# A two-layer trunk on one core: the first layer's MLP in phases, with ten pairs of hidden blocks by seven block products over both token halves

## The chip, the core and the metric

The kernel runs on one core of a Trainium2 chip. Its engines are TensorE (PE, with its weight loads PEld), VectorE (DVE), ScalarE (ACT), GpSimd (POOL) and SyncE (SP, which issues most DMAs). The metric is the device time of one launch in microseconds (us); lower is better.

## The reference

Tokens x (1, 1024, 1024) go through a layer with an mLSTM mixer and an MLP, then through a layer with latent attention and an MLP; a shared K/V is made between. All is float32. Cut to what the change touches:

```python
# layer 0
x = x + gate * rmsnorm(mlstm_mixer(modulate(rmsnorm(x, g), shift, scale), ...), g)
h = modulate(rmsnorm(x, g), shift, scale)
x = x + gate * rmsnorm(jnp.square(jax.nn.relu(h @ mlp_w1[0])) @ mlp_w2[0], g)   # 1024 -> 4096 -> 1024
# shift, scale, gate: columns of silu(c) @ ada_w + ada_b, one row for all tokens
# shared K/V from x, then layer 1: the same frame around causal latent attention, and an MLP
```

## The kernel before, in words

Activations stand transposed, features on 128 partitions and tokens along the row, in two token halves of 512 (`hfs[0]`, `hfs[1]`; H = 512). A float32 product is done as three matmuls (`mm3`, L230): each operand is split into a rounded part `hi` and a rest `lo`, and lo*hi, hi*lo and hi*hi are added in PSUM. A weight block of 128x1024 (512 KB) is loaded into a `raw` buffer (a ring of four that weights, background loads and others share), `wsplit` casts it on ScalarE (L189, `wh`) and subtracts on VectorE (L190, `wl`).

`mlp` (L941) walks a list of steps. A `hidden` step makes one block of 128 hidden features for a half: 8 x 3 matmuls of 128x512 into one PSUM tile `ps`, then ReLU and square on ScalarE and a split. An `up` step multiplies hidden blocks by the second weight and adds into y: 24 matmuls into `pm`, and two additions of 128x1024 (L198). Loads run two steps ahead (AHEAD). The generator yields "within" in the middle of a step and a step's name at its end.

Other work is placed between steps by generators. `go` makes each instruction of TensorE follow the one before it in the program's order, so TensorE's list is fixed. `two_streams(dense, other, fill)` runs `other`; where that yields a number n it lets the dense stream go on for 2n half steps. When the dense stream ends first, the rest of `other` is run with nothing between. `behind(fill, per)` is such an `other`: it takes `per` steps of `fill` and then yields 1.

Background work: the modulation rows (shift, scale, gate) are sums over c times ada_w. `ada_chunk` (L346 on) makes one of 512 columns: four loads of 512 KB, one multiply (L358) and seven dependent multiply-adds (L360) on VectorE into `tma` (one buffer), then four transposes on TensorE (L340) and a reduce (L342). `bg_latent` holds the sums for the shared K/V and `latent_weights` (L1130): six blocks folded with scale and shift, whose shift sums are transposed at L1154 and reduced at L1155. `bg_rest` holds four parts of two sums each for layer 1.

In layer 0, half 0's MLP `mlp(0, hfs[0], z0, [4]*8)` runs first, its first 20 yields beside `post` of half 1 (residual and norm, `p1`), the rest beside `bg_latent`. Half 1's MLP `mlp(0, hfs[1], z1, [2]*14+[4])` is the dense stream beside `mixer1` of half 0, which is half 0's latent attention, with `bg_rest` as fill. There the attention's scores (L1325 to L1331), softmax and the transposes of the probabilities (L1445) have one dense step, 24 matmuls, between scores and transposes.

## Time and profile before

| what | value |
|---|---|
| times of three runs | 2396.41, 2397.75, 2398.75 us |
| median | 2397.75 us |
| span of the profiled execution | 2395.7 us (2.05 us less than the median) |
| granted TensorE clock, mean | 0.997 |
| busy PE, DVE, ACT, POOL | 2364.8, 1550.3, 1054.9, 18.3 us |
| DMA | 374 MB, mean 156 GB/s |

The page gives for each engine its busy time and its share of the span. The page's span starts at the first instruction and ends with the last; the runs' time includes what lies around it. Matmuls overlap in the pipeline, so a group's mean duration is longer than the step from one start to the next. In a row of the groups stand line, engine, operation, names out<-in, shapes, count, then busy us, mean ns, and the idle time before with what ended it.

### The profile page before, as it was taken

How to read it: one execution, taken by the hardware profiler on the slowest of the kernel's cores; microseconds unless marked ns; L12 is line 12 of the kernel's file. 1: busy time of each engine (PE TensorE's matmuls, PEld its weight loads, DVE VectorE, ACT ScalarE, POOL GpSimd, SP SyncE). 2: the span in 40 equal slices, each digit the busy share in tenths (PEclk: the TensorE clock that was granted, in tenths of full speed). 3: DMA queues.
4: the chain of work that ended last, by engine and by line, in shares of the span. 5: the costliest groups of instructions: out<-in, count | busy, mean ns of one | idle time of the engine just before them, and what ended most of it. 6: DMA issues, size and time to landing. Idle time of an engine off the chain costs nothing.

```text
span 2395.7 us, 30518 instructions
## 1 busy us (share of the span) xinstructions
PE 2364.8 (99%) x11621; PEld 1945.5 (81%) x11621; DVE 1550.3 (65%) x2431; ACT 1054.9 (44%) x1712; POOL 18.3 (1%) x91
## 2 busy tenths in 40 slices
PE   7999999999999999999999999999999999999998
PEld 5888888788888887888888877888888888888886
DVE  6667866858656677877764867766566386353345
ACT  4355334655333454444444554344444353443333
POOL 1000000000000000000000000000000000000000
PEclk9999999999999999999999999999999999999999
DMA  8442654544654745545543444864424354354431
GB/s 310 148 143 81 192 178 134 165 132 150 189 171 152 243 138 179 159 160 186 168 137 114 153 162 153 260 240 133 139 97 150 105 167 128 101 189 140 144 99 62
DMA packets 377106, 374.48 MB, mean 156 GB/s; under 512 B 24355, under 2 KB 282464, under 8 KB 376960
## 3 DMA queue, kind: packets, MB, share of 16 engines
q1 hardware_dynamic: 376672, 372.44, 48.9%
q8 instruction: 91, 1.49, 0.3%
q14 instruction: 55, 0.45, 0.1%
q0 software_dynamic: 288, 0.10, 0.0%
HBM read 313.24 MB, written 59.24 MB: 155 GB/s over the span
## 4 chain that ended last, share of the span: by engine, by line
PE 91%; DVE 4%; DMA 3%; ACT 1%; issue 1%; SPq 0%; DVEq 0%; ACTq 0%
PE ps L231 17%; PE ps L232 17%; PE ps L233 17%; PE pm L231 10%; PE pm L232 10%; PE pm L233 10%; PE pc L1445 1%; PE pc L231 1%; PE pc L233 1%; PE pc L232 1%; PE pm L815 1%; PE pm L1331 1%; DMA raw<-in_mlp_w_dram 1%; DVE wl L190 1%; PE pm L1325 1%
## 5 line engine op out<-in xcount | busy, mean ns | idle before, releaser
L190 DVE TENSOR_TENSOR wl<-raw,wh 128x1024 fp32r<-128x1024 f32 (+2 forms) x366 | 438.7, 1202 | 449.5 <-ACT wh L189 442.3
L189 ACT CAST wh<-raw 128x1024 fp32r<-128x1024 f32 (+2 forms) x366 | 376.0, 1032 | 717.0 <-PE ps L231 392.2
L231 PE MATMUL ps<-k,wl 128*128 128x512 f32 x1528 | 611.0, 400 | 2.3 <-ACT k L671 1.4
L233 PE MATMUL ps<-k,wh 128*128 128x512 f32 x1528 | 601.0, 393 | 0.0
L232 PE MATMUL ps<-k,wh 128*128 128x512 f32 x1528 | 600.9, 393 | 0.0
L231 PEld LDWEIGHTS ps<-k,wl 128*128 128x128 f32 x1528 | 287.0, 188 | 69.7 <-issue 2.9
L233 PEld LDWEIGHTS ps<-k,wh 128*128 128x128 f32 x1528 | 287.0, 188 | 67.3 <-issue 0.5
L232 PEld LDWEIGHTS ps<-k,wh 128*128 128x128 f32 x1528 | 287.5, 188 | 63.6 <-issue 1.7
L198 DVE TENSOR_TENSOR k<-k,pm 128x512 f32<-128x512 f32 (+1 forms) x254 | 210.9, 859 | 107.0 <-PE pm L233 106.5
L231 PE MATMUL pm<-hd,wl 128*128 128x512 f32 x512 | 202.0, 394 | 0.4 <-ACT hd L470 0.4
L233 PE MATMUL pm<-hd,wh 128*128 128x512 f32 x512 | 199.8, 391 | 0.0
L232 PE MATMUL pm<-hd,wh 128*128 128x512 f32 x512 | 199.5, 390 | 0.2 <-DVE hd L471 0.2
L231 PE MATMUL pm<-wh,hd 128*128 128x512 f32 x488 | 192.9, 395 | 3.2 <-ACT raw L1337 2.9
L232 PE MATMUL pm<-wl,hd 128*128 128x512 f32 x488 | 191.3, 392 | 0.0
L233 PE MATMUL pm<-wh,hd 128*128 128x512 f32 x488 | 190.3, 390 | 0.0
L360 DVE SCALAR_TENSOR_TENSOR tma<-raw,cond,tma 128x512 f32<-128x512 f32 x168 | 125.6, 747 | 20.6 <-DMA raw<-in_kv_ada_w_dram 14.6
L471 DVE TENSOR_TENSOR hd<-tmp,hd 128x512 fp32r<-128x512 f32 x128 | 88.3, 690 | 56.8 <-ACT hd L470 56.5
L1337 ACT ACTIVATE raw<-pm,sm 128x128 f32<-128x128 f32 (+3 forms) x64 | 47.5, 742 | 151.3 <-DVE sm L1336 122.7
L232 PEld LDWEIGHTS pm<-hd,wh 128*128 128x128 f32 x512 | 96.2, 188 | 21.3 <-DVE hd L471 0.5
L231 PEld LDWEIGHTS pm<-hd,wl 128*128 128x128 f32 x512 | 96.1, 188 | 21.2 <-ACT hd L470 0.8
L233 PEld LDWEIGHTS pm<-hd,wh 128*128 128x128 f32 x512 | 96.1, 188 | 21.1
L231 PEld LDWEIGHTS pm<-wh,hd 128*128 128x128 f32 x488 | 91.6, 188 | 24.9 <-ACT raw L1337 5.5
(347 smaller groups left out, 3414.5 us busy)
## 6 DMA issues: line engine op xcount, KB each, us to landing
raw<-in_mlp_w_dram SPq DMA_DIRECT2D x256, 512.0 KB, 4.1
raw<-in_ada_w_dram SPq DMA_DIRECT2D x80, 512.0 KB, 4.3
raw<-in_a_w_in_dram SPq DMA_DIRECT2D x48, 512.0 KB, 4.1
xs<-k SPq DMA_DIRECT2D x40, 256.0 KB, 4.8
raw<-in_kv_ada_w_dram SPq DMA_DIRECT2D x16, 512.0 KB, 3.8
raw<-in_a_w_out_dram SPq DMA_DIRECT2D x16, 512.0 KB, 4.6
kd<-k SPq DMA_DIRECT2D x32, 256.0 KB, 3.7
vd<-k SPq DMA_DIRECT2D x32, 256.0 KB, 5.0
```

Of the source, the lines that this page charges most:

```text
L189: nc.scalar.copy(hi[:, :n], r[:, :n])
L190: i = nc.vector.tensor_sub(lo[:, :n], r[:, :n], hi[:, :n].bitcast(F32))
L198: return f(*a, **k)
L231: nc.tensor.matmul(o, ll, rh, start=start, stop=False)
L232: nc.tensor.matmul(o, lh, rl, start=False, stop=False)
L233: pe_last[0] = nc.tensor.matmul(o, lh, rh, start=False, stop=stop)
L360: nc.vector.scalar_tensor_tensor(acc, r[:, kk], cond[:, k : k + 1], acc, ALU.mult, ALU.add)
L471: nc.vector.tensor_sub(lo, u, hi.bitcast(F32))
L815: nc.tensor.matmul(nv[:, r, i], hf.PT[p_][:, r, cs], v[:, 2 * p_ + r], start=g == 0, stop=True,)
L1325: nc.tensor.matmul(o[:, :w], ql, kh, start=True, stop=False)
L1331: nc.tensor.matmul(o[:, :w], qh, kh, start=False, stop=True)
L1337: nc.scalar.activation(pr[:, :n], f, AF.Exp, bias=m, scale=SCALE, accum_out=l)
```

## The change

Layer 0's MLP is done in phases.

(A) `up_front` makes the first six pairs of hidden blocks (ALONE = 6, twelve blocks) of half 0 as before and stores each block in DRAM (`hidd`). Beside it runs `post` of half 1, two steps of it for each step, which now also forms sums and differences of the two halves' normed operands (`kept1`) for phase B and stores two tiles in DRAM (`b12`).

(B) `seven` makes the other ten pairs for both halves at once. A pair's product with both halves is seen as 2 x 2 blocks (two hidden blocks, or the two halves of features, by two token halves) and done with seven block products in place of eight, 7 x 12 = 84 matmuls of 128x512 in place of 96. Weight sums (L1009 to L1017 of the new program) and sums of results (L1036, L1044, L1046) are formed on VectorE. After each product one step of the background work `bgl` (`bg_latent`, then `bg_rest`) is taken. Results go to `hidd`.

(C) The down product of half 0 reads the hidden blocks from `hidd` (`mlp(..., stored=True)`, 32 steps of 24 matmuls, `f2`), beside `behind(bgl, 1)`. `with_b12` gets the stored tiles back.

(D) Half 1's MLP, `up_front` of six pairs and then the stored down product, is the dense stream beside `mixer1` of half 0, with `bgl` as fill. The attention yields 0.5 in place of 1: half a dense step, 12 matmuls.

Counted in the two programs: 120 fewer matmuls of 128x512 (11,283 matmuls in all, 11,403 before), 70 more instructions on VectorE, 4 more on ScalarE, and 92 more DMAs issued by SyncE (44 stores to and 64 fetches from `hidd`, 4 for `b12`, 20 fewer weight loads).

What stands in a row, at two places of the program. Names are buffers with numbers; [waits X] names whose semaphores the row waits for.

The first place is the end of half 0's MLP, and the background sums around it. TensorE before: here a sum (tma_1345) of `bg_rest`, beside half 1's MLP.

```order
L232 MATMUL pm_1388_8185<-hd_1290_7648,wh_1357_8027 128x512
L233 MATMUL pm_1388_8185<-hd_1290_7648,wh_1357_8027 128x512
L231 MATMUL pm_1388_8185<-hd_1353_7994,wl_1358_8028 128x512
L232 MATMUL pm_1388_8185<-hd_1353_7994,wh_1357_8027 128x512
L231 MATMUL pc_1376_8125<-k4_1364_8069,wl_1331_7912 128x512 [waits Activation_49]
L233 MATMUL pm_1388_8185<-hd_1353_7994,wh_1357_8027 128x512
L340 MATMUL pc_1389_8199<-ident_64,tma_1345_7971 128x128 [waits DVE_49]
L340 MATMUL pc_1389_8199<-ident_64,tma_1345_7971 128x128 x3
L232 MATMUL pc_1376_8125<-k4_1365_8070,wh_1330_7911 128x512 [waits DVE_49]
L233 MATMUL pc_1376_8125<-k4_1364_8069,wh_1330_7911 128x512
L231 MATMUL pc_1376_8125<-k4_1364_8069,wl_1331_7912 128x512 [waits Activation_49]
```

TensorE after, from the last two matmuls of half 0's down product (pm_1400) to the first two of half 1's hidden blocks (ps_1463):

```order
L233 MATMUL pm_1400_8134<-k4_1386_8002,wh_1395_8074 128x512
L234 MATMUL pm_1400_8134<-k4_1385_8001,wh_1395_8074 128x512
L341 MATMUL pc_1401_8160<-ident_64,tma_1379_7989 128x128 [waits DVE_49]
L341 MATMUL pc_1401_8160<-ident_64,tma_1379_7989 128x128 x3
L341 MATMUL pc_1408_8185<-ident_64,tma_1403_8168 128x128 [waits DVE_49]
L341 MATMUL pc_1408_8185<-ident_64,tma_1403_8168 128x128 x3
L341 MATMUL pc_1415_8210<-ident_64,tma_1410_8193 128x128 [waits DVE_49,PE_49]
L341 MATMUL pc_1415_8210<-ident_64,tma_1410_8193 128x128 x3
L341 MATMUL pc_1422_8235<-ident_64,tma_1417_8218 128x128 [waits DVE_49,PE_49]
L341 MATMUL pc_1422_8235<-ident_64,tma_1417_8218 128x128 x3
L232 MATMUL ps_1463_8320<-k4_1286_7509,wl_1456_8305 128x512 [waits DVE_49]
L233 MATMUL ps_1463_8320<-k4_1287_7510,wh_1455_8304 128x512 [waits Activation_49]
```

Four sums' transposes now stand one after another between the two dense streams, where one stood among matmuls.

VectorE before, part of the sum tma_1345 above, with the MLP's operations (L471, L198, L190) between:

```order
L360 SCALAR_TENSOR_TENSOR tma_1345_7971<-raw_1348_7980,cond_85,tma_1345_7971 128x512 [waits DVE_49]
L360 SCALAR_TENSOR_TENSOR tma_1345_7971<-raw_1349_7984,cond_85,tma_1345_7971 128x512 [waits DMAHW4_49,DVE_49]
L471 TENSOR_TENSOR hd_1353_7994<-tmp_1355_8020,hd_1353_7994 128x512 [waits Activation_49]
L360 SCALAR_TENSOR_TENSOR tma_1345_7971<-raw_1349_7984,cond_85,tma_1345_7971 128x512 [waits DVE_49]
L198 TENSOR_TENSOR k4_1208_7286<-k4_1208_7286,pm_1359_8031 128x1024 [waits PE_49,Pool_49]
L190 TENSOR_TENSOR wl_1352_7991<-raw_1350_7988,wh_1351_7990 128x1024 [waits DMAHW5_49,Activation_49]
L198 TENSOR_TENSOR k4_1209_7287<-k4_1209_7287,pm_1360_8045 128x1024 [waits PE_49,Pool_49]
L190 TENSOR_TENSOR wl_1358_8028<-raw_1356_8025,wh_1357_8027 128x1024 [waits DMAHW6_49,Activation_49]
```

VectorE after, the third of the four sums (tma_1410), from the reduce of the second to its own:

```order
L343 TENSOR_REDUCE sm_1409_8190<-pc_1408_8185 128x4 [waits PE_49]
L359 TENSOR_SCALAR tma_1410_8193<-raw_1411_8194,cond_85 128x512 [waits DMAHW4_49,DVE_49]
L344 TENSOR_TENSOR ada_104<-sm_1409_8190,cols_95 128x4 [waits DVE_49]
L361 SCALAR_TENSOR_TENSOR tma_1410_8193<-raw_1411_8194,cond_85,tma_1410_8193 128x512 [waits DVE_49]
L387 SCALAR_TENSOR_TENSOR mods_106<-ada_104,cols_95 128x8 [waits DVE_49]
L361 SCALAR_TENSOR_TENSOR tma_1410_8193<-raw_1412_8198,cond_85,tma_1410_8193 128x512 [waits DMAHW5_49,DVE_49]
L361 SCALAR_TENSOR_TENSOR tma_1410_8193<-raw_1412_8198,cond_85,tma_1410_8193 128x512 [waits DVE_49]
L361 SCALAR_TENSOR_TENSOR tma_1410_8193<-raw_1413_8202,cond_85,tma_1410_8193 128x512 [waits DMAHW6_49,DVE_49]
L361 SCALAR_TENSOR_TENSOR tma_1410_8193<-raw_1413_8202,cond_85,tma_1410_8193 128x512 [waits DVE_49]
L361 SCALAR_TENSOR_TENSOR tma_1410_8193<-raw_1414_8206,cond_85,tma_1410_8193 128x512 [waits DMAHW7_49,DVE_49]
L361 SCALAR_TENSOR_TENSOR tma_1410_8193<-raw_1414_8206,cond_85,tma_1410_8193 128x512 [waits DVE_49]
L343 TENSOR_REDUCE sm_1416_8215<-pc_1415_8210 128x4 [waits PE_49]
```

The sum's operations stand without dense operations between, and its reduce waits for TensorE.

The second place is the start of half 0's down product, and the folding of the latent weights around it. TensorE before, one transpose of `latent_weights` beside half 0's MLP:

```order
L233 MATMUL pm_1144_6817<-hd_1067_6336,wh_1127_6723 128x512
L231 MATMUL pm_1144_6817<-hd_1077_6409,wl_1128_6724 128x512
L232 MATMUL pm_1144_6817<-hd_1077_6409,wh_1127_6723 128x512
L233 MATMUL pm_1144_6817<-hd_1077_6409,wh_1127_6723 128x512
L1154 MATMUL pc_1145_6843<-ident_64,tma_1132_6758 128x128 [waits DVE_49]
L231 MATMUL ps_1154_6871<-k4_732_4342,wl_1137_6777 128x512 [waits DVE_49]
L232 MATMUL ps_1154_6871<-k4_733_4343,wh_1136_6776 128x512 [waits Activation_49]
```

TensorE after, from the last of the seven-product matmuls (ps_1107) to the first of the down product (pm_1165):

```order
L232 MATMUL ps_1107_6561<-k4_822_4852,wl_1093_6415 128x512
L233 MATMUL ps_1107_6561<-k4_823_4853,wh_1092_6414 128x512
L234 MATMUL ps_1107_6561<-k4_822_4852,wh_1092_6414 128x512
L1327 MATMUL pc_1120_6656<-ident_64,tma_1117_6627 128x128 [waits DVE_49]
L1327 MATMUL pc_1144_6746<-ident_64,tma_1123_6675 128x128 [waits DVE_49]
L232 MATMUL pm_1165_6871<-k4_1136_6710,wl_1134_6706 128x512 [waits DVE_49]
L233 MATMUL pm_1165_6871<-k4_1137_6711,wh_1133_6705 128x512 [waits Activation_49]
L234 MATMUL pm_1165_6871<-k4_1136_6710,wh_1133_6705 128x512
L232 MATMUL pm_1165_6871<-k4_1136_6710,wl_1134_6706 128x512
```

VectorE after, from the first transpose's reduce to the subtraction (wl_1134) that row pm_1165 waits for:

```order
L1328 TENSOR_REDUCE lbias_135<-pc_1120_6656 128x1 [waits PE_49]
L1317 TENSOR_SCALAR tma_1123_6675<-raw_1121_6659,ada_104 128x128 [waits DMAHW7_49]
L490 TENSOR_TENSOR k4_1131_6699<-raw_1129_6697,k4_1130_6698 128x1024 [waits DMAHW6_49,Activation_49]
L1319 SCALAR_TENSOR_TENSOR tma_1123_6675<-raw_1121_6659,ada_104,tma_1123_6675 128x128 [waits DVE_49] x7
L1322 TENSOR_TENSOR raw_1121_6659<-raw_1121_6659,mods_106 128x1024 [waits DVE_49]
L1328 TENSOR_REDUCE lbias_135<-pc_1144_6746 128x1 [waits PE_49]
L490 TENSOR_TENSOR k4_1137_6711<-raw_1135_6709,k4_1136_6710 128x1024 [waits DMAHW4_49,Activation_49]
L190 TENSOR_TENSOR wl_1125_6686<-raw_1121_6659,wh_1124_6685 128x1024 [waits Activation_49]
L190 TENSOR_TENSOR wl_1134_6706<-raw_1132_6703,wh_1133_6705 128x1024 [waits DMAHW2_49,Activation_49]
```

Two transposes stand next to each other where 48 matmuls lay between two, and VectorE has a whole folding (tma_1123), two fetched splits (k4_1131, k4_1137) and the first down weights between them and the down product.

The diff, cut to its core:

```diff
+    def up_front(l, hf, pairs):
...
+        def hidden(f):
+            def hid(w):
...
+                    nc.scalar.activation(s, pt, AF.Relu)
+                    nc.scalar.activation(s, s, AF.Square)
+                    nc.sync.dma_start(hidd[hf.i, f // 2][:, ts(f % 2, 512)], s)
...
+    def seven(l, pairs, B, out):
...
+        def load(p_):
+            with tc.high_priority(PRIO):
+                r1, r2 = raw(), raw()
+                for r, f in ((r1, 2 * p_), (r2, 2 * p_ + 1)):
+                    nc.sync.dma_start(r.rearrange("p (a b) -> p a b", b=P), wcols(w1, f * P))
...
+                A = wsplit(r1, 1024)
+                t1, t2 = raw(), raw()
+                nc.vector.tensor_add(t2[:, lo_], r2[:, lo_], r2[:, hi_])
+                nc.vector.tensor_sub(t1[:, hi_], t2[:, lo_], r1[:, lo_])
...
+        def product(u, i):
...
+            for k in range(4):
+                mm3(o, wh[:, k], wl[:, k], bh[k], bl[k], i in (1, 2, 7) and k == 0, k == 3, more=i not in (1, 2, 7))
...
+            for u, i in ((cur, 1), (prev, 5), (cur, 2), (prev, 4), (cur, 6), (prev, 3), (cur, 7)):
+                if u:
+                    product(u, i)
+                    yield "hid"
+            prev = cur
...
-    def mlp(l, hf, y, sizes, rows=False):
+    def mlp(l, hf, y, sizes, rows=False, stored=False):
...
+        def fetch(f):
+            with tc.high_priority(PRIO):
+                r, hi, lo = raw(), k4v(F32R), k4v(F32R)
+                nc.sync.dma_start(r, hidd[hf.i, f // 2])
+                split_wide(hi, lo, r.rearrange("p (a b) -> p a b", b=512))
...
+        if stored:
+            fetch(0)
+            fetch(2)
+            steps = []
+            for g in range(NF // 4):
+                for i in range(4):
+                    load, run = up(list(range(4 * g, 4 * g + 4)), i, g == NF // 4 - 1)
+
+                    def both(load=load, f=4 * g + 2 * i):
+                        w = load()
+                        if i >= 2 and f < NF:
+                            fetch(f)
+                        return w
+
+                    steps.append((both, run))
...
-        yield 1
+        yield (0.5, 1)[hf.i]
...
-            yield 2
+            yield 1
...
-                hf, groups, cycle((1,)),
+                hf, groups, cycle((0.5,)),
...
-    f0 = mlp(0, hfs[0], z0, [4] * 8)
-    for n in range(20):
-        if next(f0) != "within":
+    for v in up_front(0, hfs[0], range(ALONE)):
+        if v != "within":
+            next(p1, None)
             next(p1, None)
     drain(p1)
-    two_streams(f0, behind(bg_latent(), 4))
+    bgl = chain(bg_latent(), bg_rest())
+    traced = nc.cur_bb.bb.instructions
+    z0 = FH()
+    f2 = mlp(0, hfs[0], z0, [], stored=True)
+    f0, n = seven(0, range(ALONE, NF // 2), blocks, both_halves), 0
+    while go(f0) is not end:
+        pace[0] = next(i for i in reversed(traced) if i.engine == dve)
+        n += 1
+        next(bgl, None)
+        if n == 7 * (NF // 2 - ALONE) - 5:
+            next(f2)
...
+    two_streams(with_b12(f2), behind(bgl, 1))
     rope_perm()
...
-    two_streams(mlp(0, hfs[1], z1, [2] * 14 + [4]), mixer1(hfs[0], z0, attention_first), bg_rest())
+    two_streams(
+        chain(
+            up_front(0, hfs[1], range(ALONE)),
+            (v for v in mlp(0, hfs[1], z1, [], stored=True) if v != "primed"),
+        ),
+        mixer1(hfs[0], z0, attention_first), bgl,
+    )
```

More of the change, by code (lines that the diff above doesn't have):

```diff
@@ L939, with ahead_of @@
     AHEAD = 2
-    def mlp(l, hf, y, sizes, rows=False):
+    hidd = scratch([2, NF // 2, P, 2 * H], "hidd")
+    def ahead_of(steps, primed=False):
+        ready = []
+        for n in range(len(steps) + AHEAD):
+            if primed and n == AHEAD:
+                yield "primed"
+            if n < len(steps):
+                ready.append(steps[n][0]())
+            if n >= AHEAD:
+                yield from steps[n - AHEAD][1](ready.pop(0))
+                yield steps[(n - AHEAD + 1) % len(steps)][1].__name__
@@ new lines, in both_halves, with done @@
+    def both_halves(p_):
+        o, s = Half(), [k4v(), hdv()]
+        o.c = [[s[0][:, 0], s[1][:, 0]], [s[0][:, 1], s[1][:, 1]]]
+        def done():
+            nc.vector.tensor_scalar(s[0], s[0], 0.0, None, ALU.max)
+            nc.vector.tensor_scalar(s[1][:, 1], s[1][:, 1], 0.0, None, ALU.max)
+            for i in range(2):
+                nc.scalar.activation(s[i], s[i], AF.Square)
+                nc.sync.dma_start(hidd[i, p_], s[i].rearrange("p a b -> p (a b)"))
+        o.done = done
+        return o
@@ L1046, in mlp @@
         up = up_rows if rows else up_cols
+        if stored:
[11 more added lines that the diff above has]
+                    steps.append((both, run))
+            n = 0
+            for v in ahead_of(steps, True):
+                if v == "primed":
+                    yield v
+                    continue
+                n += v != "within"
+                yield v if v == "within" else "hid"
+            return
         steps, prev, f0 = [], [], 0
@@ L1757, in post @@
         yield 0
+        if kept:
+            yield from kept(y, rstd)
+            return
         hf.h2 = Split()
@@ L1764, with kept0 @@
     )
-    p0 = post(hfs[0], y0, B0, x_ahead(k4v, True), A1, adac(0, SH2))
+    def kept0(y, rstd):
+        hfs[0].h2 = Split()
+        h = hfs[0].h2
+        yield from normed_kept(y0, rstd, A1, adac(0, SH2), list(zip(h.hi.t, h.lo.t)))
+    p0 = post(hfs[0], y0, B0, x_ahead(k4v, True), A1, adac(0, SH2), kept0)
     so = split_o(hfs[1])
```

159 lines of the change are left out of this document (142 added, 17 removed).

## The prediction

> **What bounds the kernel now.** I read the page's totals and the chain of waits first, then windows of 100 us, then TensorE's waits, and last timelines of the stretches whose pieces the change re-uses. The first fence holds the totals and the chain by engine, the second windows (span, then busy us of PE, PEld, DVE, ACT, POOL with counts; granted clock; DMA share; GB/s), the third TensorE's longest waits (total, times, longest).
>
> ```profile
> PE 2364.8 (99%) x11621; PEld 1945.5 (81%) x11621; DVE 1550.3 (65%) x2431; ACT 1054.9 (44%) x1712; POOL 18.3 (1%) x91
> PE 91%; DVE 4%; DMA 3%; ACT 1%; issue 1%; SPq 0%; DVEq 0%; ACTq 0%
> ```
>
> ```profile
> 0.00:100.00 100.00, 86.87 (x458) 67.14 (x459) 62.33 (x118) 38.09 (x60) 7.31 (x26) 0.97 0.75 254
> 500.00:600.00 100.00, 100.00 (x435) 81.03 (x434) 83.26 (x120) 56.88 (x79) 0.55 (x4) 1.00 0.48 151
> 600.00:700.00 100.00, 100.00 (x448) 81.96 (x447) 64.94 (x85) 36.79 (x48) 0.00 (x0) 1.00 0.63 194
> 1000.00:1100.00 100.00, 99.72 (x522) 83.72 (x521) 75.52 (x129) 46.13 (x84) 0.82 (x4) 1.00 0.58 180
> 1500.00:1600.00 100.00, 99.61 (x477) 82.75 (x476) 65.70 (x101) 40.19 (x63) 0.20 (x1) 1.00 0.79 264
> 2300.00:2396.00 96.00, 87.17 (x382) 71.18 (x380) 46.87 (x78) 30.46 (x55) 0.00 (x0) 0.97 0.23 77
> ```
>
> ```profile
> PE pc L527 <- DMA k<-in_x_dram: 4.4, 4, 1.5
> PE pm L231 <- ACT k L473: 4.4, 1, 4.4
> ```
>
> TensorE is the bound and has no slack to give: of its 30.9 us idle, 13.1 lie in the first 100 us and 8.8 in the last 96, and no wait between is over 4.4 us. So every matmul removed is time gained, and every wait added to TensorE is time lost, one for one.
>
> **What the change removes.** After the change TensorE's list holds 120 fewer matmuls of 128x512 (11,283 for 11,403): ten pairs at 84 for 96. Their price is not the mean duration. The first row below gives that mean (400 ns), the others, TensorE's timeline of 24 such matmuls, give the starts.
>
> ```profile
> L231 PE MATMUL ps<-k,wl 128*128 128x512 f32 x1528 | 611.0, 400 | 2.3 <-ACT k L671 1.4 <-DVE wl L190 0.8
> 1052.79 0.39 PE L231 MATMUL ps<-k,wl 128*128 128x512 f32 x1
> 1053.02 0.39 PE L232 MATMUL ps<-k,wh 128*128 128x512 f32 x1
> ...
> 1058.36 1.04 PE L1445 MATMUL pc<-ident,raw 128*128 128x128 f32 x8
> ```
>
> Twenty-four starts take 1058.36 − 1052.79 = 5.57 us, 0.232 us each: the durations overlap. The gain is 120 × 0.232 = **27.8 us**, not the 48 that 0.400 would give. Also from this: 12 matmuls are 2.78 us, a round of 84 is 19.5 us.
>
> **Prices for what is added.** VectorE's timeline of one background sum, then its groups for operand splits and weight folding, then the loads.
>
> ```profile
> 654.71 0.68 DVE L342 TENSOR_REDUCE sm<-pc 128x4 f32<-128x512 f32 x1
> 655.31 0.48 DVE L358 TENSOR_SCALAR tma<-raw,cond 128x512 f32<-128x512 f32 x1
> 655.70 0.15 DVE L343 TENSOR_TENSOR ada<-sm,cols 128x4 f32<-128x4 f32 x1
> 655.82 0.75 DVE L360 SCALAR_TENSOR_TENSOR tma<-raw,cond,tma 128x512 f32<-128x512 f32 x1
> 658.25 1.23 DVE L190 TENSOR_TENSOR wl<-raw,wh 128x1024 fp32r<-128x1024 f32 x1 [1.68 <-ACT wh L189]
> 659.40 3.11 DVE L360 SCALAR_TENSOR_TENSOR tma<-raw,cond,tma 128x512 f32<-128x512 f32 x4
> 509.72 4.73 DVE L927 SCALAR_TENSOR_TENSOR k<-k,mods,tmc 128x512 f32<-128x512 f32 x7
> 518.57 2.50 DVE L930 TENSOR_TENSOR k<-k,hd 128x512 f32<-128x512 f32 x4
> L1146 DVE SCALAR_TENSOR_TENSOR tma<-raw,ada,tma 128x128 f32<-128x128 f32 x21 | 7.4, 352 | 0.7
> L1149 DVE TENSOR_TENSOR raw<-raw,mods 128x1024 f32<-128x1024 f32 x6 | 7.3, 1225 | 0.2
> L1155 DVE TENSOR_REDUCE lbias<-pc 128x1 f32<-128x128 f32 x6 | 1.7, 283 | 0.0
> raw<-in_mlp_w_dram SPq DMA_DIRECT2D x256, 512.0 KB, 4.1
> raw<-in_ada_w_dram SPq DMA_DIRECT2D x80, 512.0 KB, 4.3
> ```
>
> Start to start that is about 1.15 us for a subtraction of 1024 columns (658.25 to 659.40), 0.77 for a dependent multiply-add of 512 (3.11 / 4), 0.67 for an independent one (4.73 / 7), 0.61 for an add of 512 (2.50 / 4), 0.6 for the reduce, 0.4 for the first multiply.
>
> **1. End of half 0's down product: +26.** The stored `mlp` gives 32 steps, and `behind(bgl, 1)` takes one background step at each: about 4.6 of the eight sums of `bg_rest`. The rest is drained by the same call after the dense work has ended, and the order on record shows it: after the last matmul of pm_1400 TensorE has nothing but four groups of transposes until ps_1463, and each needs a sum that VectorE does after the group before it (tma has one buffer). On VectorE from the last matmul: the addition 1.15, a reduce 0.6, then three sums of 0.4 + 7 × 0.77 = 5.8 each with small operations between (7.1 the first, which has two adds of 512 in it, 6.0 and 5.9 the others), after each about 0.8 for the transposes and the way to TensorE and back and 0.6 for the reduce, and 1.15 for wl_1456 at the end: 1.75 + 19.0 + 3 × 1.4 + 1.15 = 26.1. Before, these sums lay beside half 1's MLP; that cover is gone. Bounds: 22 (no tiny operations between), 31 (12 loads through the four-slot raw ring at 4.3 us, if they don't stay ahead).
>
> **2. From the products to the down product: +8.7.** The first two latent-weight transposes stand behind the last product. Between them and the next matmul VectorE has, in order, a reduce 0.28, a multiply 0.2, a subtraction 1.15, seven multiply-adds of 128x128 at most 0.352 each (0.27 by their pitch), a product of 1.15, a reduce 0.28, and three subtractions of 1.15: 8.4, and 0.3 for the way. Before, 48 matmuls stood between such transposes. Bounds 8 and 9.5.
>
> **3. First steps of the down product: +5.5.** Up to the third step's weights (wl_1161) VectorE has some 14.4 us of folding and splits by the same prices, TensorE 48 matmuls, 11.1 us and two short transposes; then two fetched halves of `hidd` each 1.15 late. 3 to 8.
>
> **4. From plain pairs to products: +4.2.** From post's last column sum to the operand half hd_847 VectorE's list holds 24 operations of 1024, ten adds and ten multiply-adds of 512: 24 × 1.15 + 6.1 + 6.7 + 0.5 = 40.9 us; TensorE has 157 matmuls, 36.4. Bounds 0 (post runs ahead by that much) and 8.
>
> **5. The seven products: +6.** Per pair VectorE has about 16 of TensorE's 20.0 us (19.5 and four background transposes), so it isn't the bound. The ring is: three or four pieces of a round go through one slot after another (a load 4.1, a split 1.15, and again, behind a wait for VectorE's turn), about 21 us against 20. One us lost in each of five rounds with background loads; bounds 0 and 17 (3.4 each, if a load takes 5). The 64 stores and fetches of `hidd` and b12 add DMA work that the window of 600 to 700 at 194 GB/s leaves room for.
>
> **6. Down product, steady: +2.** Per 5.57 us it takes about 2.6 loads of 512 KB: a weight, a background load, and a fetch at nearly every step, since `fetch` in `both` reads `i` when it is called, and that is 3 then: 32 fetches a half where 16 are needed. That is about 245 GB/s; 254 to 264 occurs in the windows above, with TensorE at 99.6 in the later one. Bounds 0 and 10.
>
> **7. Thin filler: +3.** Twelve matmuls (2.78 us) now stand between scores and transposes. In the trace scores end at 1052.79 and VectorE's last probability scaling is the second row here:
>
> ```profile
> 1055.41 0.28 DVE L1339 TENSOR_SCALAR raw<-raw,sm 128x128 f32<-128x128 f32 x1
> 1056.58 0.35 DVE L1339 TENSOR_SCALAR raw<-raw,sm 128x256 f32<-128x256 f32 x1
> ```
>
> It ends at 1056.93, 4.1 us after the scores: 24 matmuls cover that, 12 leave 1.4. There are four such places, four more with heavier scores; without background multiply-adds between, VectorE comes about 1.5 us sooner. Bounds 0 and 10.
>
> **8. Clock: +3.** The windows with 13.1 and 8.8 us idle show 0.97, so about 3 us of full-speed work lost in each; all others show 1.00. The gap of step 1 is longer than either, though broken by transposes. Bounds 0 and 6. [...]
>
> **The sum.** −27.8 + 26.0 + 8.7 + 5.5 + 4.2 + 6 + 2 + 3 + 3 = +30.6. The profiled span is 2395.7, the median of the runs 2397.75, so 2.05 lie around the span, taken as unchanged. 2397.75 + 30.6 gives **2428 us**, 1.3% slower.
>
> **Rivals.**
> - *Faster: the leftover sums stay hidden.* It turns on one place: if the three sums ran beside the last steps of the down product, step 1 falls from 26 to 2, and with the small terms at their low ends (8 + 3) the time is 2397.75 − 27.8 + 13 = 2383. It takes a step-1 gap under about 14 us to end faster. For it: VectorE is only 65% busy. Against: the order puts every one of those sums behind the addition of pm_1400. 0.06.
> - *No change:* steps 1 and 2 near their bounds (22 + 8) and all else hidden: 2397.75 − 27.8 + 30 = 2400. For it: 35% of VectorE is free, and TensorE lost under 0.5 us in each of the four windows above that lie between the ends. 0.10.
> - *Loads bind:* steps 5 and 6 at their upper ends, 27 instead of 8, and 5 us more in step 1: 2452. For it: the ring has four slots and the loads of a round are serial; against: TensorE stayed at 99.6 while 264 GB/s moved. 0.18.
> - The forecast itself, 2405 to 2442: 0.66.
>
> A measurement of this kernel can tell about 0.2%, 4.8 us, from no change. The no-change case reaches 2393 to 2402.5. Below that lies 0.06, above it 0.84. The range of 8 in 10 is 2402 to 2453: from the no-change case's edge to the case of binding loads.
>
> **What would show it.** After: TensorE with 120 fewer matmuls; a hole of 22 to 31 us with four small groups of transposes right after the first half's down product, VectorE on line 361 throughout; before the down product a hole of 8 to 10 with line 1327's transposes; rounds of 20 to 21 us in the products; waits at line 1618 of 0.5 to 1.5. I would be wrong if the line 361 sums run beside matmuls at that place, or if products take over 23 us a round.

## The result, and the profile after

The changed kernel takes 2509.2 us (median of four runs, 2507.1 to 2515.4), the kernel before 2397.4 on the same chip: 1.046 times as long, 95% interval 1.045 to 1.048, or 112 us more. The forecast was 2428, and its range ended at 2453.

The totals of the profile after, in the same form as before:

```profile
span 2505.0 us, 30646 instructions
PE 2374.4 (95%) x11501; PEld 1938.9 (77%) x11501; DVE 1623.3 (65%) x2501; ACT 1086.4 (43%) x1708; POOL 17.3 (1%) x83
```

(ScalarE ran 1708 instructions, four fewer than before and not four more as counted ahead.) The span grew by 109.3 us. TensorE's idle time, span less busy time, grew from 30.9 to 130.6: 99.7. Its busy time grew too, by 9.6, though it has 120 matmuls fewer, worth 27.8 at 0.232: the remaining ones took 37.4 us longer. These two numbers, 99.7 of waits and 37.4 of slower matmuls, are what has to be explained.

Five of the windows of 100 us show where (span, busy us and counts of PE, PEld, DVE, ACT, POOL, granted clock, DMA share, GB/s):

```profile
500.00:600.00 100.00, 93.63 (x397) 75.14 (x395) 76.84 (x95) 54.36 (x77) 0.00 (x0) 0.97 0.44 140
700.00:800.00 100.00, 83.49 (x345) 65.84 (x344) 81.20 (x137) 47.58 (x56) 0.00 (x0) 0.91 0.64 211
800.00:900.00 100.00, 88.86 (x371) 70.19 (x369) 72.87 (x87) 37.50 (x37) 0.00 (x0) 0.93 0.77 251
1000.00:1100.00 100.00, 73.58 (x307) 58.16 (x306) 64.56 (x95) 33.45 (x52) 0.00 (x0) 0.85 0.60 191
1400.00:1500.00 100.00, 88.63 (x358) 70.00 (x357) 74.59 (x87) 40.75 (x51) 0.39 (x4) 0.91 0.62 200
```

TensorE is idle for 100.9 us between 500 and 1500 us, in the phases of the new program, so all of the growth lies there. The granted clock, which was 1.00 everywhere between the ends, is now under 1.00 in each of these five windows.

TensorE's longest waits (engine, line, what it waited for: total, times, longest):

```profile
PE pc L341 <- DVE tma L361: 22.0, 3, 8.4
PE pm L232 <- ACT k L489: 10.6, 3, 5.4
PE pm L232 <- ACT raw L1510: 10.2, 12, 1.3
PE ps L232 <- DVE wl L190: 9.7, 4, 4.5
PE pm L232 <- ACT k L202: 9.1, 1, 9.1
PE pm L232 <- DVE k L198: 8.7, 7, 2.7
PE ps L233 <- DVE hd L490: 6.3, 1, 6.3
PE ps L232 <- ACT hd L1048: 6.1, 3, 2.9
PE pm L232 <- DVE wl L190: 5.9, 1, 5.9
PE pm L233 <- DVE k L490: 5.9, 4, 4.0
PE pc L1327 <- DVE tma L1319: 5.5, 1, 5.5
```

Before, the longest was 4.4 us. Line 341 is the hole that the prediction put at the end of the first half's down product. TensorE's timeline there (start, duration, engine, line, operation, idle time before and what ended it), with the next hidden block's matmuls behind it:

```profile
1010.51 1.12 PE L341 MATMUL pc<-ident,tma 128*128 128x128 f32 x4 [8.41 <-DVE tma L361]
1018.41 1.09 PE L341 MATMUL pc<-ident,tma 128*128 128x128 f32 x4 [6.78 <-DVE tma L361]
1026.27 1.09 PE L341 MATMUL pc<-ident,tma 128*128 128x128 f32 x4 [6.78 <-DVE tma L361]
1031.82 0.80 PE L232 MATMUL ps<-k,wl 128*128 128x512 f32 x1 [4.46 <-DVE wl L190]
1032.41 0.63 PE L233 MATMUL ps<-k,wh 128*128 128x512 f32 x1
1032.84 0.63 PE L234 MATMUL ps<-k,wh 128*128 128x512 f32 x1
...
1035.83 0.40 PE L233 MATMUL ps<-k,wh 128*128 128x512 f32 x1
1036.06 0.39 PE L234 MATMUL ps<-k,wh 128*128 128x512 f32 x1
```

The four waits are 8.41 + 6.78 + 6.78 + 4.46 = 26.4 us. The 26.1 that had been forecast were the whole hole, transposes included, and that is 30.2 us, from 1001.66 to 1031.82, near the upper bound of 31. Two rows of VectorE show what was sized too small:

```profile
1011.66 0.69 DVE L343 TENSOR_REDUCE sm<-pc 128x4 f32<-128x512 f32 x1 [1.21 <-PE pc L341]
1030.54 1.23 DVE L190 TENSOR_TENSOR wl<-raw,wh 128x1024 fp32r<-128x1024 f32 x1 [2.25 <-ACT wh L189]
```

The way to TensorE and back took 1.21 to 1.27 us three times, not 0.8, and before the last subtraction VectorE waited 2.25 us for a cast. Behind the hole the matmuls start 0.43 us apart, not 0.23, until 1035.4. That second part is the new one.

### The profile page after: what moved, and what is told of

It is laid out like the page before. It is cut to its first block, busy times and chain, and to the rows that moved or that the text cites. A ratio compares the mean times of both kernels' runs of the same rounds, so it can differ in the third digit from the quotient of the medians.

```text
span 2505.0 us, 30646 instructions
## 1 busy us (share of the span) xinstructions
PE 2374.4 (95%) x11501; PEld 1938.9 (77%) x11501; DVE 1623.3 (65%) x2501; ACT 1086.4 (43%) x1708; POOL 17.3 (1%) x83
## 3 DMA queue, kind: packets, MB, share of 16 engines
q8 instruction: 91, 1.49, 0.2%
## 4 chain that ended last, share of the span: by engine, by line
PE 73%; DMA 11%; DVE 9%; ACT 3%; issue 2%; SPq 0%; DVEq 0%; ACTq 0%
PE ps L232 14%; PE ps L233 13%; PE ps L234 13%; PE pm L232 7%; PE pm L233 7%; PE pm L234 7%; DMA raw<-hidd 4%; DMA raw<-in_mlp_w_dram 3%; DVE wl L190 2%; DMA raw<-in_ada_w_dram 1%; DVE k L490 1%; DVE tma L361 1%; PE pc L1618 1%; ACT k L489 1%; PE pc L233 1%
## 5 line engine op out<-in xcount | busy, mean ns | idle before, releaser
L190 DVE TENSOR_TENSOR wl<-raw,wh 128x1024 fp32r<-128x1024 f32 (+2 forms) x356 | 427.2, 1201 | 424.7 <-ACT wh L189 405.2
L232 PE MATMUL ps<-k,wl 128*128 128x512 f32 x1328 | 534.1, 402 | 18.9 <-DVE wl L190 9.7
L234 PE MATMUL ps<-k,wh 128*128 128x512 f32 x1328 | 524.3, 395 | 0.0
L233 PE MATMUL ps<-k,wh 128*128 128x512 f32 x1308 | 517.0, 395 | 0.0
L232 PEld LDWEIGHTS ps<-k,wl 128*128 128x128 f32 x1328 | 250.9, 189 | 82.1 <-ACT hd L1048 7.7
L232 PE MATMUL pm<-k,wl 128*128 128x512 f32 x636 | 261.2, 411 | 47.1 <-ACT k L489 10.6
L234 PEld LDWEIGHTS ps<-k,wh 128*128 128x128 f32 x1328 | 251.1, 189 | 58.8 <-issue 0.5
L233 PEld LDWEIGHTS ps<-k,wh 128*128 128x128 f32 x1308 | 247.5, 189 | 54.9 <-issue 2.2
L233 PE MATMUL pm<-k,wh 128*128 128x512 f32 x636 | 256.5, 403 | 5.9 <-DVE k L490 5.9
L234 PE MATMUL pm<-k,wh 128*128 128x512 f32 x636 | 255.0, 401 | 0.0
L198 DVE TENSOR_TENSOR k<-k,pm 128x512 f32<-128x512 f32 (+1 forms) x226 | 177.0, 814 | 77.6 <-PE pm L234 77.0
L232 PEld LDWEIGHTS pm<-k,wl 128*128 128x128 f32 x636 | 122.9, 193 | 82.4 <-ACT k L489 12.2
L233 PEld LDWEIGHTS pm<-k,wh 128*128 128x128 f32 x636 | 123.3, 194 | 37.3 <-DVE k L490 7.8
L234 PEld LDWEIGHTS pm<-k,wh 128*128 128x128 f32 x636 | 122.9, 193 | 28.5
L490 DVE TENSOR_TENSOR k<-raw,k 128x1024 fp32r<-128x1024 f32 x66 | 80.5, 1224 | 52.4 <-ACT k L489 51.4
L232 PEld LDWEIGHTS pm<-wh,hd 128*128 128x128 f32 x488 | 91.6, 188 | 23.6 <-ACT raw L1510 4.5
L234 PEld LDWEIGHTS pm<-wh,hd 128*128 128x128 f32 x488 | 91.6, 188 | 20.7 <-issue 0.5
```

What stands on the lines that cost most here:

```text
L190: i = nc.vector.tensor_sub(lo[:, :n], r[:, :n], hi[:, :n].bitcast(F32))
L198: return f(*a, **k)
L232: nc.tensor.matmul(o, ll, rh, start=start, stop=False, **m)
L233: nc.tensor.matmul(o, lh, rl, start=False, stop=False, **m)
L234: pe_last[0] = nc.tensor.matmul(o, lh, rh, start=False, stop=stop, **m)
L490: nc.vector.tensor_sub(lo, u, hi.bitcast(F32))
```

## The experiments

Theory A after the result: TensorE's waits come from fetches, loads and sums that stand in the wrong order, and each wait of about two us or more costs 1.3 to 2.7 us again (p1_probe measured these, below), because the matmuls behind it run at half rate (a start each 0.43 us for 0.23, as behind the hole above). Rivals: the slower matmuls come from load traffic (C); the queue of loads sets the start of the down product whoever fetches (B); what is taken from one place only delays another (D).

### One index, and the leftover sums

**e1_bind.** The function that loads a step read `i` when it was called; here it keeps its own.

```diff
-                    def both(load=load, f=4 * g + 2 * i):
+                    def both(load=load, f=4 * g + 2 * i, i=i):
```

> Change: the inner function of the stored down product keeps its own i, so each half fetches 16 tiles of hidden blocks in place of 32. Theory A (late and doubled fetches are what TensorE waits for at the starts and ends of both down products): of the waits on lines 489, 490 and 202 (10.6 + 5.9 + 9.1 us) some 15 to 20 go, with them the half-rate stretches behind them, 5 to 8 us: 2509 falls to 2482 to 2490. Rival B (SyncE's queue holds the loads behind the stores of the folded weights, whoever fetches what): under 8 us, 2501 to 2509.

Measured 2467.3 us (1.0285 times before): 42 less than the changed kernel, where theory A expected 19 to 27. Fetches fell from 64 to 32, TensorE's idle time from 130.6 to 103.3, and its busy time by 10.4. The profile of this run:

```profile
PE pm L232 <- ACT k L202: 7.9, 1, 7.9
PE pm L232 <- ACT k L489: 2.1, 1, 2.1
PE pm L232 <- DVE k L198: 0.8, 1, 0.8
PE 2364.0 (96%) x11501; PEld 1936.3 (78%) x11501; DVE 1585.2 (64%) x2469; ACT 1054.9 (43%) x1676; POOL 17.5 (1%) x83
raw<-hidd SPq DMA_DIRECT2D x32, 512.0 KB, 4.3
```

The waits for fetched casts (line 489) fell from 10.6 to 2.1 us, those for line 198, in the steady down products, from 8.7 to 0.8. By place, 6.7 us in half 0's down product and 11.4 at the end of half 1's became 0 and 0.8. One stayed, the 9.1 us for line 202, now 7.9: there rival B is right. In the changed kernel's timeline of SyncE's queue it reads so:

```profile
795.66 3.92 SPq L354 DMA_DIRECT2D raw<-in_ada_w_dram  x2
805.35 0.34 SPq L1324 DMA_DIRECT2D lw<-wh  x1
...
807.03 0.55 SPq L1324 DMA_DIRECT2D lw<-wl  x1
813.33 0.34 SPq L1324 DMA_DIRECT2D lw<-wh  x1
813.77 0.37 SPq L1095 DMA_DIRECT2D raw<-hidd  x1
```

From 799.6 to 805.3 and from 807.6 to 813.3 the queue issues nothing: each time a store of folded weights (line 1324) waits for its cast on ScalarE, 5.7 us, and a load of the down product stands behind it. The load from 813.8 is the one whose cast holds up line 202 on ScalarE until 820.

**e2_rest.** The down product takes one background step per step and stops; what is left of `bgl` goes on as fill beside the attention.

```diff
-    two_streams(with_b12(f2), behind(bgl, 1))
+    down = with_b12(f2)
+    while (v := go(down)) is not end:
+        pace[0] = next(i for i in reversed(traced) if i.engine == dve)
+        if v == "hid":
+            some(bgl, 1)
+    pace[0] = None
```

> Change: the background sums that are left when half 0's down product ends are not drained there but go on as fill beside the attention of half 0. Theory A (a wait costs itself and then some 1.8 us of half-rate matmuls per piece): 26.4 us of waits before the transposes of line 341 and before line 232 go, and 5 to 8 us of half rate: 2474 to 2479. Rival C (the longer matmuls come from load traffic, not from waits): 26 us only, 2483. Rival D (the sums delay the attention instead, with thin filler): 10 us or less gained, 2499 or more.

Measured 2482.1 us (1.035): 27 less. The waits on line 341 are gone. But the gain lies below theory A and is no proof of half rate, since other waits grew: those on line 489 from 10.6 to 16.3, on line 1327 from 5.5 to 8.8, of pm on line 190 from 5.9 to 10.6. Part of D is true: the moved sums cost some of it elsewhere.

**e3_both.** Both edits.

> Both edits. If the two causes are separate the gains add: 2509 minus 24 minus 33 is 2452 (2445 to 2462). If the sums fill the place that the fetches freed, or the other way, less than the sum by over 8 us.

Measured 2445.5 us (1.019): 63.7 less, where the two alone give 42 and 27. The gains nearly add, as they should if the two causes are separate.

### Thin filler

**e4_thick.** On top of e3_both, the attention of half 0 yields 1 and 2 again in place of 0.5 and 1.

> Both edits, and the attention of half 0 yields 1 and 2 again in place of 0.5 and 1 (24 matmuls between scores and transposes). If thin filler costs what the trace shows as waits on line 1510, 198 and 1638 between 1160 and 1345 us, 10 to 11 us: 10 us under e3_both. Rival: these waits sit behind ScalarE, which the thick filler doesn't relieve, or half 1's stream ends before the attention does: within 4 us of e3_both, or slower.

Measured 2485.8 us: 40 us slower than e3_both. Its waits:

```profile
PE pc L462 <- DVE tmc L458: 24.4, 2, 21.8
PE pm L232 <- ACT raw L1510: 10.7, 12, 1.4
```

With thick filler half 1's stream ends before half 0's last norm, which then stands bare (21.8 us at once, and more behind it). Thick filler costs more than the thin one does: the thin one keeps cover for the end. And the waits on line 1510 stay at 12, though the filler is twice as long: filler isn't what they lack. More on this below.

### Half rate behind a wait

**p1_probe.** In the last dense stretch of the kernel before, ten times:

```diff
+            pt = pc()
+            nc.tensor.transpose(pt[:, :P], ident, ident)
+            t = tmc()
+            nc.vector.tensor_copy(t[:, :P], pt[:, :P])
+            for _ in range(m):
+                nc.vector.tensor_scalar(t[:, :P], t[:, :P], 1.0, None, ALU.mult)
+            p2 = pc()
+            pe_last[0] = nc.tensor.transpose(p2[:, :P], t[:, :P], ident)
```

> The kernel before, with ten probes in its last dense stretch, where TensorE is otherwise never idle: a 128x128 transpose, then a chain of 0, 3, 5, 7, 9, 11, 13, 16, 20 and 26 dependent VectorE operations of 128x128, then a transpose that needs its end. TensorE is idle for about 0.7 to 6 us at each. Theory A (each idle time above some length is followed by a stretch of half rate of fixed length): starts of the 128x512 matmuls behind the long probes are 0.43 us apart for about 3.5 us and 0.23 after; behind the short ones 0.23 at once; the length from which it begins lies between 1.4 and 2.1 us, as the gaps of the changed kernel suggest, and each probe above it costs its idle time plus 1.7. [...] Rival C: no half rate behind any (the stretches of the changed kernel come from load traffic).

One run, 2470.7 us. TensorE was idle for 0.38, 2.31, 2.50, 8.12, 5.11, 4.90, 4.52, 6.21, 8.34 and 8.73 us at the ten places (other VectorE work fell into the chains). Behind the first the starts are 0.23 us apart at once, behind the second too. Behind each of the other eight, 6 to 13 starts are 0.43 apart, and these lose 1.3 to 2.7 us against 0.232, 14.9 together. The first rows show the start of the one behind 4.9 us. The others show the granted clock (behind span, busy us and count of PE; then DMA share, GB/s) around the waits of 2.31 us, which ends at 2083.23, and of 2.50 us, which ends at 2115.01:

```profile
2226.57 0.45 PE L1939 MATMUL pc<-ident,tmc 128*128 128x128 f32 x1 [4.90 <-DVE tmc L1937]
2227.24 0.63 PE L232 MATMUL pm<-wl,hd 128*128 128x512 f32 x1
2227.66 0.63 PE L233 MATMUL pm<-wh,hd 128*128 128x512 f32 x1
```

```profile
2078.77:2082.19 3.42, 2.15 (x10) 1.00 0.74 216
2082.19:2085.60 3.41, 2.37 (x11) 1.00 0.40 109
2112.91:2116.32 3.41, 1.31 (x7) 1.00 0.26 77
2116.32:2119.73 3.41, 3.41 (x10) 0.50 0.00 0
```

Here no phase, product or fetch is in play, and in the last row the DMA share is 0.00: rival C falls for these. And half rate is the granted clock, 0.50 in that row. In the changed kernel's trace the eleven stretches at 0.50 between 480 and 1560 us last 3.41 us (five of them) to 30.72 us, each a whole number of times 3.41, and the stretches at 1.00 between them, 10.24 to 283.30 us, are such multiples too. The waits show no sharp length from which it begins. The wait of 2.31 us lies in the first two of the four rows above, each with over 2 us of work, and no half rate followed. The wait of 2.50 us lies but for its first 0.4 us in the third row, with 1.31 us of work, and the next row is at 0.50, so that half rate began 1.3 us after work had resumed. In the changed kernel it came with waits of 2.03 and 2.08 us too: TensorE was busy for 1.38 and 1.32 of the 3.41 us ahead of the stretches at 0.50 that begin at 1444.92 and 622.31.

### The boundary, and the operand half

Three edits on top of e3_both, and all together. **e5_quiet**: the last eight products take no background step (`if n <= 7 * (NF // 2 - ALONE) - 8: next(bgl, None)`).

> On top of e3_both (2445.5): the last eight products take no background step, so that the folding of the latent weights falls beside the down product. Theory A (a wait costs itself and about 1.8 us of half rate behind it): the waits of 5.6, 4.3 and 5.5 us at the start of the down product and three half-rate pieces go, 19 to 21 us: 2424 to 2428. Rival B (SyncE's queue: the stores of folded weights now hold back the loads inside the down product): 10 us or less, 2435 or more.

Measured 2441.5 us: 4 less, not 20. The waits of 5.6, 4.3 and 5.5 us at the down product's start became 3.2 and 1.8, but 3.5 and 0.7 appear at its end, and at two places in the attention waits of 3.0 us stand where e3_both had 2.2 and none: the steps that had been moved. Theory A had named the right waits and forgotten that the work has to go somewhere.

**e6_prime**: half 1's stored down product is started one step before the last hidden block.

> On top of e3_both: in half 1's stream the first loads and fetches of the stored down product are issued one step before the last hidden block, not after it. Theory A: the waits of 2.1 and 3.0 us at its start and one half-rate piece of 1.8 go, 6 to 7 us: 2438 to 2440. Rival: the casts wait for something else there (ScalarE is held by the attention), under 3 us: 2443 or more.

Measured 2442.9 us (2440.8 to 2444.8): 2.6 less than e3_both, on the rival's side, and too near to tell. The two waits that theory A named are gone; others of 3.2 us (weights, line 190) and 1.7 us (line 1618) stand in the attention instead.

**e7_alone7**: `ALONE = 7`.

> On top of e3_both: seven pairs alone and nine by products, so 12 more matmuls (2.8 us) and two more blocks beside post of half 1. Theory A: the wait of 6.3 us for the operand half and its half-rate piece of 1.8 go, net 5: 2440; the shift of the background sums by seven steps also moves the latent transposes, so up to 10 more may go. Rival: VectorE is late by its own backlog and only 2 us go, which the added matmuls eat: 2445 to 2447.

Measured 2436.2 us: 9.3 less, with 2.8 of matmuls more. As theory A had it: the 6.3 us are gone, and the waits at the start of the down product fell from 15.3 to 7.9. But half 1's down product now waits 12.0 us for its first weights.

**e8_all**: the three together.

> All three on top of e3_both. If they are independent: 2445.5 minus 20, 6 and 5 is 2414 (2408 to 2420). It would still be above the kernel before by 12 to 18 us: 28 saved, about 10 left in the products, 12 in the attention and some 15 of half rate and tails.

Measured 2430.7 us: 14.9 less than e3_both, where the three alone give 16.0. Of the 31 expected, e5's share was the one most missed. That the gains nearly add doesn't show that they are independent: the 12.0 us of e7_alone7 are gone here, since e6_prime's edit starts those loads earlier.

### The ring of loads

**e9_raw5.** Five buffers in the ring, not four (`RAW = 5`, `TMC = 5`, `TMP = 2`), on top of e3_both.

> On top of e3_both: five buffers in the ring of loads, not four (one tmp and one tmc fewer to make room). If the serial ring is what the products wait for: the four waits of 1.4 to 2.4 us in the products go, with two half-rate pieces, and those of 4.3 and 5.5 us at the start of the down product shrink: 12 to 16 us less, 2430 to 2434. If VectorE's and ScalarE's order is the cause: within 4 us of 2445.5, or slower for want of tmp and tmc.

Measured 2431.9 us: 13.7 less, the size that was expected for the ring; TMP and TMC changed with it. TensorE's waits in the profile of e3_both, then the same of e9_raw5:

```profile
PE ps L232 <- ACT hd L1048: 6.6, 3, 2.4
PE pc L1327 <- DVE tma L1319: 5.5, 1, 5.5
```

```profile
PE ps L232 <- ACT hd L1048: 2.7, 1, 2.7
PE pc L1327 <- DVE tma L1319: 2.4, 1, 2.4
```

ScalarE's ReLU on line 1048, which frees a product's PSUM tile, stood behind a cast. At 622 us in e3_both that cast waited for VectorE's sum of two loaded pieces, the sum for its load, and the load's issue for buffers that VectorE still read. But the place of the gain is not the expected one alone: the waits within the products fell from 8.7 to 6.1 us only, those at the start of the down product from 15.3 to 11.5, and TensorE's busy time fell by 5.3. A rival for what is left there is untested: in the products of e3_both SyncE's queue waits 47 us in all for the stores of hidden blocks (line 1081), up to 7.7 at once, and no run put these stores on another queue.

**e10_all5.** The same on top of e8_all.

> On top of e8_all (2430.7): five buffers in the ring. If the ring is the cause of the waits that are left in the products (2.8, 2.1 and 3.0 us) and in the down product (3.3): 2430.7 minus 11 and four half-rate pieces of 1.7 is 2413. Otherwise within 4 us of 2430.7.

Measured 2410.8 us (1.0047 times before, 1.0031 to 1.0062): 19.9 less, near the 2413 expected, though 6.2 us of waits stay in the products, 3.7 of them at once. This is the best version found; it is still slower than the kernel before. Its totals, span 2410.0 us:

```profile
PE 2352.5 (98%) x11513; PEld 1929.1 (80%) x11513; DVE 1575.8 (65%) x2460; ACT 1054.6 (44%) x1678; POOL 17.9 (1%) x83
```

Of the 98.4 us that it is faster than the changed kernel by its medians, the profiles give 73.1 to idle time (130.6 to 57.5) and 21.9 to busy time, though it has 12 matmuls more.

**e11_eight.** On top of e3_both, product 2 of each pair is computed twice: 120 matmuls more, the result the same.

> On top of e3_both: one of the seven products is computed twice, 120 matmuls more, as many as plain products need, with everything else as it is. If TensorE is the bound in the products apart from fixed waits: 27.8 us more, 2473. If the products have a floor set by the ring of loads and the order of ScalarE and VectorE (rounds of 21 to 22 us whatever TensorE does): the waits of 9 us and their half-rate pieces of 5 are filled first, and it costs 12 to 18 only: 2458 to 2464. The difference to 27.8 is the part of the saving that the products never gave.

Measured 2467.9 us: 22.4 more. Between the two theories, nearer to TensorE as the bound: about 5 of 27.8 us had been lost to the products' own waits, not 10 to 16. So the block products do give most of their saving, and most of the loss lies around them.

### The waits on line 1510

**e12_own.** On top of e10_all5, half 1's stored product accumulates in single-bank PSUM tiles (`ps`), not in the double ones (`pm`) of the attention's scores.

```diff
-                        b2 = pm()
+                        b2 = None if stored and hf.i else pm()
...
-                    pt = b2[:, m % 2]
+                    pt = b2[:, m % 2] if b2 is not None else ps()
```

> On top of e10_all5 (2410.8): half 1's stored down product accumulates in two single-bank PSUM tiles (ps), not in the double tiles (pm) that the attention's scores use, and adds 512 columns at a time. If the waits on line 1510 are for a PSUM tile that the softmax still reads, not for want of filler: the nine waits of 0.9 to 2.8 us there (12 us with tails) go: 2397 to 2401. If they are want of filler: they turn up before the transposes of line 1618 instead, gain under 4 us: 2407 or more. A third way: ps is shared with the attention's products, and the waits move there: 2403 to 2411.

Measured 2427.7 us, 17 slower than e10_all5. Its waits, and ahead of them the one of e10_all5 that it was to remove:

```profile
PE pm L232 <- ACT raw L1510: 12.4, 12, 2.8
```

```profile
PE ps L232 <- DVE k L198: 10.4, 5, 3.5
PE ps L232 <- DVE k L472: 6.3, 5, 4.6
PE pc L1620 <- DVE raw L1514: 5.6, 7, 1.6
```

The waits for the softmax's exponentials (line 1512 here) fell from 12.4 to 1.8 us, so most were for a PSUM tile that it still read. But `ps` tiles wait longer for VectorE, and the transposes (line 1620 here) now wait 5.6 in all, 2.7 in e10_all5, which may be the thin filler's own share.

**e15_own5.** The same for the first 20 of the 32 steps only.

> On top of e10_all5 (2410.8): as e12_own, but only the first 20 of the 32 steps of half 1's stored down product, those beside the attention proper, use the single-bank tiles; the last 12 go back to the double ones. e12_own took the waits on line 1510 away and put waits of 4.6, 3.5, 2.9 and 2.3 us for ps tiles behind VectorE's norms in their place, after the attention. If those come only from the steps after it: they go, and the waits on line 1510 stay away: 2401 to 2406. If ps tiles make the attention itself wait (2.7 us at its start, the 4.6 at its end): 2409 or more.

Measured 2417.9 us: 7 slower than e10_all5. The wait of 4.6 us is at the attention's own end, as the rival had it.

### Where to put the sums

**e13_own_loud**, e12_own without the pause; **e14_spread**, e12_own with one pause after every seventh product instead; **e16_more**, e15_own5 with eight more background steps beside half 0's down product.

> e12_own without the pause of background steps in the last eight products. In e5_quiet the pause gave 4 us where 20 were expected, since the sums then crowded the down product and the attention. With five buffers: if the boundary's folding chain still costs the 2.4, 4.2 and 4.8 us of e9_raw5, 8 to 14 us slower than e12_own; if seven pairs alone have moved the folding off the boundary, faster than e12_own by 2 to 5.

> e12_own with the pause spread: no background step after every seventh product, nine fewer in all. If the rounds of the products are bound by loads in the ring (four background loads a round), the waits of 1.2, 1.2 and 3.7 us there go: 5 to 8 us under e12_own. If the boundary matters more, the folding is back there: slower than e12_own by 2 to 10.

> e15_own5 with eight more background steps beside half 0's down product (one more at every fourth step), so fewer are left for the first attention, where e10_all5 waits 4 us before the transposes of line 1618 and VectorE does leftover sums. If the sums delay that softmax: 4 to 7 us faster than e15_own5. If the down product has no room for them (it waits 0.7 and 2.4 us as it is): the same or slower.

Measured 2430.3 (2426.4 to 2433.9), 2442.0 and 2420.5 us: the first within 3 us of e12_own (2427.7), which neither theory had, the second 14 slower, more than expected, the third 2.5 slower than e15_own5, as its rival had it. e14 shows again waits of 3.1, 2.3 and 5.3 us at the boundary and behind it. None of the places tried takes the sums for nothing.

## Why the prediction was wrong

The direction was right; the size was not: 30.6 us were forecast and 112 measured. Two steps failed. Step 6 saw the doubled fetches and priced them at 2 us, by bandwidth; e1_bind, which removes them and changes nothing else, took 42 us away. And step 8 put the clock at 3 us, where matmuls took 37.4 us longer: the premise that a wait added to TensorE is lost one for one doesn't hold. By its steps, each against TensorE's waits in the profile after:

- *Matmuls saved, −27.8*: right in count and pitch; e11_eight gives 22.4 for as many, so about 5 were lost inside the products.
- *1, the leftover sums, 26*: 26.4 of waits in a hole of 30.2. The place and the cause were right; that the two numbers meet is luck in part, since the 26.1 held the transposes.
- *2, the latent weights, 8.7*: 5.5 + 5.9 = 11.5.
- *3, first steps of the down product, 5.5*: 11.2, of which 9.1 are one wait. The step counted VectorE's work and left out SyncE's queue, where stores that wait stand ahead of loads, and ScalarE's, where an evacuation of PSUM stood behind a cast that waited for a fetch.
- *4, the operand half, 4.2*: 6.3. Its own terms give 40.9 − 36.4 = 4.5. *5, the products, 6*: 9.4. One us in each of five rounds is 5, not 6. The reason, the serial ring, is shown for a part only (e9_raw5).
- *6, steady down product, 2*: 6.7. In half 0's down product the doubled fetches cost this, and in half 1's the 11.4 us below; without them both are under 1 us (e1_bind). At the end of half 1's this was order and not bandwidth: while TensorE waits there, from 1476 to 1482 us, the DMA share is 0.31. In half 0's, with a share of 0.77 from 800 to 900 us, no run tells the two apart.
- *7, thin filler, 3*: 11.5, over the bound of 10 and for another reason: 8.4 of it is the wait on line 1510, for a PSUM tile (e12_own). The waits that the step had in mind, before the transposes of line 1618, are 0.4 us in all.
- *Not in the sum at all*: 17.5 us around half 1's stored product (5.0 at its start, 1.1 later, 11.4 at its end). The prediction spoke of that phase for its filler only, and put these at nothing without a reason.
- *8, clock, 3*: matmuls took 37.4 us longer. The granted clock says how much of that is the clock. Between 480 and 1560 us it is at 0.50 in eleven stretches. The first row is the sum over them (us, busy PE), the second the one stretch of the kernel before with matmuls in it:

```profile
sum 102.41, PE 51.29; mean PE 4.66
24.57:31.39 6.82, 3.36 (x7) 0.50 1.05 387
```

Half of the busy time is lost, so by estimate 25.6 us, and before 1.7. The prediction had read 0.97 over 100 us as 3 us of work lost; but TensorE was idle for half of that stretch, and behind 2390 us there was nothing left to slow down. Behind a wait p1_probe shows 1.9 us lost in the mean of eight. The mistake was to have one new gap in mind, that of step 1: the timeline has 16 waits of 2 us or more between 480 and 1560 us, some so near each other that they share a stretch. The rest, about 12 us, is at the edges of some 45 waits: the last matmul ahead of one counts as busy for 0.39 us where it takes 0.23 when another follows, and behind a short one the first start is 0.34 ahead of the next (869.21 to 869.55), which makes 0.27 each by estimate.

So the terms of waits held 55 of 100 us, and the clock 3 of 37: of the 79 us missed between the two profiles, 45 are waits and 34 slower matmuls. The case of binding loads (2452) was nearest and still 57 short. It had one right mechanism, the ring, in it, but not the queue's order, and a wait was priced once where it is often paid again behind it.

What stays open: whether the saving can be kept at all. The best arrangement tried, 2410.8, keeps TensorE idle for 26.6 us longer than the kernel before, and its busy time is 12.3 lower where 25.0 fewer us of matmuls would allow. Nor did any run move the waiting stores to another queue. That products are the wrong choice here isn't shown; that these phases leave too little dense work around the sums is what the runs suggest.

## What to carry to other kernels

Saving matmuls on a bound engine pays only if nothing loses its cover: list what the removed or moved work had hidden (here background sums, a fold, a norm), and follow every queue in its order, also that of the engine that only issues loads (here a load stood twice behind a store that waited 5.7 us). Price a wait of TensorE of two us or more above its length: in p1_probe eight such waits lost 1.3 to 2.7 us more behind them, 1.9 in the mean, and one of 2.31 us nothing. And read late-bound loop variables in code that builds programs as schedule bugs: the results stay right, and 42 us are lost.

## What the runs showed of the hardware

In the changed kernel's trace 16 waits of TensorE of 2 us or more lie between 480 and 1560 us. Eleven of them, of 2.03 to 9.12 us, begin at a granted clock of 1.00, and with or behind each a stretch at 0.50 begins; the other five, of 3.96 to 6.78 us, begin inside these stretches. With five waits of 1.32 to 1.36 us the clock stayed at 1.00. In the probe it was 0.50 behind the wait of 2.50 us and stayed at 1.00 with the one of 2.31. In the 3.41 us ahead of each of the eleven stretches TensorE was busy for 0.00 to 1.49 us; in the rows of p1_probe, for 1.31 us ahead of the row at 0.50, and for 2.15 and 2.37 us in the two rows of the wait that passed without. In the probe half rate lasted for 6 to 13 matmuls of 128x512 at 0.43 us, whether 2.5 or 8.7 us had been idle.
